# A gated MLP's down-projection by seven block products instead of eight

## The chip, the cores and the metric

The kernel runs on one core of a Trainium2 chip. The core has five engines with an instruction queue each: TensorE (PE in the profile; PEld is its loading of the stationary operand), VectorE (DVE), ScalarE (ACT), GpSimd (POOL) and SyncE (SP), which here only issues DMA transfers. The metric is the device time of one execution in microseconds, the median of several runs.

## The reference

One layer of an encoder: 512 tokens, 1024 channels, float32. A mixer with two branches fills the first two thirds of the kernel; the change is behind it, in the channel sublayer and the two layer norms around it:

```python
x = layer_norm(ALPHA * x + merged @ w_out[l], ln1_g[l], ln1_b[l])
u = causal_dwconv(x @ w_up[l], f_conv_w[l], f_conv_b[l])      # width 3, x is 512 x 1024, w_up 1024 x 5504
u_gate, u_val = jnp.split(u, 2, -1)                            # 512 x 2752 each
x = layer_norm(ALPHA * x + (jax.nn.silu(u_gate) * u_val) @ w_down[l], ln2_g[l], ln2_b[l])   # w_down 2752 x 1024
```

## The kernel before

**Precision.** A float32 matrix product is made of three products of a narrower float type, `fp32r`. Each operand X is split into a high part (`H`, ScalarE's cast) and a low part (`L` = X - H, a subtraction by VectorE), and TensorE adds H·H, L·H and H·L up in PSUM.

**Weights.** All weights lie in DRAM as units of 128x1024 (512 KB), in the order in which they are used. `advance(n)` keeps the stream ahead: SyncE loads `raw` up to four units ahead (`RAW_AHEAD`), and ScalarE and VectorE split units into `wH` and `wL` up to two ahead (`HL_AHEAD`); `raw`, `wH` and `wL` have rings of a few buffers. So each split waits for TensorE's last use of the buffer that it writes into.

**Up-projection.** For each of 21 blocks j of 128 channels, two units (gate and value) are multiplied into a PSUM bank each (`feature_major`, 24 matmuls of 128x512). `conv_taps` reads a bank three times (ScalarE, then two passes of VectorE), ScalarE applies silu, VectorE multiplies gate and value, and the result, channels x tokens, is split into `fH[j]` and `fL[j]`, which stay in SBUF. The last 64 channels of gate and value share one unit and one bank, `um`, and are read by the taps `cgm`.

**Down-projection.** `wide_product` holds 4 row blocks c of 128 tokens times 2 column halves hf, that is all 8 PSUM banks, `wd00` to `wd31`. For each block of 128 channels it does 24 matmuls with `fH`/`fL` as stationary operand and the split weights as moving one (`step`). The 16 first units run one after the other over all banks; the last five and the stacked 64 rows are done bank by bank, so that the row blocks end one after the other. PSUM banks come from two rings, `mm_bank` (to which `um` also belongs) and `sm_bank`.

**Around it.** After the first layer norm the normalised rows go to DRAM (`x1d`). For the residual, eight tiles `x1r[c][hf]` of 128x512 are read back ahead of the down-projection, and VectorE applies the first norm's scale `gt1[0]` and shift `gt1[1]`. When a bank is done, VectorE adds ALPHA times `x1r` (L1090) and takes statistics (L1091). `ln_finish` and `shift` make mean and deviation (GpSimd's power, L232, then `nb`, L1100), ScalarE normalises, VectorE multiplies with `gt2[0]`, GpSimd adds `gt2[1]`, SyncE stores. For the last row block, VectorE itself does most of this (L1122, L1124).

**Order.** A scheduler places the instructions on their engines; inside `in_order(*CORE)` they stand as written.

## Time and profile before

| | |
|---|---|
| median of 3 runs | 942.83 us (942.66 to 943.1) |
| profiled execution | 942.7 us, its span 941.0 us |
| granted TensorE clock | 0.994 of full speed, mean over the span |
| TensorE busy | 924.0 us of the span, 4565 matmuls |
| VectorE busy | 555.0 us, 916 instructions |
| ScalarE busy | 382.3 us |
| GpSimd busy | 66.0 us, 81 instructions |
| DMA | 105.13 MB, mean 112 GB/s |
| down-projection, first to last matmul's start | 812.69 to 931.42 us |

The busy time of an engine counts its running instructions alone. Matmuls overlap: each is shown with some 390 ns, but the next one starts earlier, so TensorE's time is best read from the distance of their starts. Rows name the engine, the line, and the tiles written and read. In this text, L numbers of the kernel before are those of its listing above; the changed kernel has its own.

### The profile page before, as it was taken

To read this page: it belongs to the slowest core of one execution; us is meant where nothing else is said; L and a number is where in the kernel's file an instruction comes from. 1 tells how busy PE (TensorE), PEld (TensorE's weight loads), DVE (VectorE), ACT (ScalarE), POOL (GpSimd) and SP (SyncE) were. 2 spreads that over 40 slices of the span, in tenths; PEclk is the share of its full clock that TensorE was granted. 3 is DMA by queue.
4 is the path that set the end of the run, shared out by engine and by line. 5 is a ranking of instruction groups with operands and counts; after the bars stand their busy time and mean duration, and the time that the engine had idled before them with its cause. 6 is when DMAs were issued, how large, how long until landed. Compare 5 with 4: busy or idle time off the path is not lost.

```text
span 941.0 us, 11703 instructions
## 1 busy us (share of the span) xinstructions
PE 924.0 (98%) x4565; PEld 762.3 (81%) x4565; DVE 555.0 (59%) x916; ACT 382.3 (41%) x572; POOL 66.0 (7%) x81
## 2 busy tenths in 40 slices
...
GB/s 186 105 101 138 109 88 142 123 147 118 90 111 70 139 109 77 102 90 96 106 112 157 112 178 91 90 90 92 109 90 93 110 90 91 251 128 90 95 62 90
DMA packets 46311, 105.13 MB, mean 112 GB/s; under 512 B 4064, under 2 KB 21144, under 8 KB 46256
## 3 DMA queue, kind: packets, MB, share of 16 engines
...
q0 software_dynamic: 512, 1.07, 0.4%
...
q14 instruction: 19, 0.16, 0.1%
...
HBM read 100.08 MB, written 4.30 MB: 111 GB/s over the span
## 4 chain that ended last, share of the span: by engine, by line
PE 94%; DVE 2%; DMA 1%; issue 1%; POOL 0%; ACT 0%; DVEq 0%; ACTq 0%; POOLq 0%
PE u L185 23%; PE wd L944 10%; PE g L185 9%; PE z L185 5%; PE o L185 5%; PE v L575 5%; PE xs L185 5%; PE pb L185 5%; PE pa L185 5%; PE wo L944 4%; PE bc L185 4%; PE q L185 2%; PE k L185 2%; PE bc L335 1%; PE up L185 1%
## 5 line engine op out<-in xcount | busy, mean ns | idle before, releaser
L165 DVE TENSOR_TENSOR wL<-raw,wH 128x1024 fp32r<-128x1024 f32 x151 | 186.4, 1238 | 231.3 <-ACT wH L159 229.2
L159 ACT CAST wH<-raw 128x1024 fp32r<-128x1024 f32 x152 | 159.1, 1051 | 285.5 <-PE g L185 62.8
L185 PE MATMUL u<-x1H,wL 128*128 128x512 f32 x312 | 121.4, 389 | 0.0
L185 PE MATMUL u<-x1L,wH 128*128 128x512 f32 x312 | 121.4, 389 | 0.0
L185 PE MATMUL u<-x1H,wH 128*128 128x512 f32 x312 | 121.4, 389 | 0.0
L185 PEld LDWEIGHTS u<-x1H,wH 128*128 128x128 f32 x312 | 58.6, 188 | 12.1
L185 PEld LDWEIGHTS u<-x1H,wL 128*128 128x128 f32 x312 | 58.6, 188 | 12.0
L185 PEld LDWEIGHTS u<-x1L,wH 128*128 128x128 f32 x312 | 58.6, 188 | 11.8
L944 PE MATMUL wd<-wH,fH 128*128 128x512 f32 x168 | 65.5, 390 | 0.8 <-ACT wH L159 0.8
L944 PE MATMUL wd<-wH,fL 128*128 128x512 f32 x168 | 65.4, 389 | 0.0
L944 PE MATMUL wd<-wL,fH 128*128 128x512 f32 x168 | 63.9, 389 | 0.0
L185 PE MATMUL g<-xnH,wH 128*128 128x512 f32 x128 | 50.1, 392 | 0.0
L185 PE MATMUL g<-xnH,wL 128*128 128x512 f32 x128 | 49.8, 389 | 0.0
L185 PE MATMUL g<-xnL,wH 128*128 128x512 f32 x128 | 49.8, 389 | 0.0
L232 POOL TENSOR_TENSOR rs<-ve,mhalf 128x1 f32<-128x1 f32 x12 | 7.6, 629 | 555.8 <-DVE ve L256 555.5
L944 PEld LDWEIGHTS wd<-wH,fH 128*128 128x128 f32 x168 | 31.5, 188 | 7.7 <-ACT wH L159 1.2
L944 PEld LDWEIGHTS wd<-wH,fL 128*128 128x128 f32 x168 | 31.5, 188 | 6.6
L944 PEld LDWEIGHTS wd<-wL,fH 128*128 128x128 f32 x168 | 31.5, 188 | 6.5
L1053 ACT CAST fH<-cg 128x512 fp32r<-128x512 f32 x21 | 13.0, 620 | 53.0 <-DVE cg L1051 53.0
L507 DVE SCALAR_TENSOR_TENSOR cv<-u,par,cv 128x511 f32<-128x511 f32 (+1 forms) x40 | 29.8, 746 | 0.7
L1050 ACT ACTIVATE cg<-cg 128x512 f32<-128x512 f32 x21 | 13.3, 632 | 40.8 <-DVE cg L507 40.8
L507 DVE SCALAR_TENSOR_TENSOR cg<-u,par,cg 128x511 f32<-128x511 f32 (+1 forms) x38 | 28.4, 746 | 0.6
...
## 6 DMA issues: line engine op xcount, KB each, us to landing
raw<-in_wts_dram SPq DMA_DIRECT2D x154, 512.0 KB, 3.3
csb<-scr SPq DMA_DIRECT2D x8, 512.0 KB, 7.3
gt<-in_prow_dram SPq DMA_DIRECT2D x12, 256.0 KB, 4.7
xt<-in_x_dram SPq DMA_DIRECT2D x4, 512.0 KB, 6.5
rb<-scr SPq DMA_DIRECT2D x4, 512.0 KB, 5.5
res<-in_x_dram SPq DMA_DIRECT2D x4, 512.0 KB, 5.3
x1d<-res SPq DMA_DIRECT2D x4, 512.0 KB, 2.6
x1r<-x1d SPq DMA_DIRECT2D x8, 256.0 KB, 5.7
```

The costliest lines, as they stand in the source:

```text
L159: nc.scalar.copy(H, raw)
L165: eng.tensor_tensor(L, raw, H.bitcast(F32), ALU.subtract)
L185: nc.tensor.matmul(ps[:, t0:t1], w_[:, k, :], a_[k][:, t0:t1], start=i == 0, stop=i == 3 * KD - 1)
L232: nc.gpsimd.tensor_tensor(dst, var, epsl[:, :n], ALU.pow)
L335: nc.tensor.matmul(fb[u][:, t], w_[:, k, :], a_[k][:, t], start=n == 1, stop=n == 3 * KD)
L507: nc.vector.scalar_tensor_tensor(dst[:, d:], ps[:, 0:T - d], prm(ws[n - 1 - d], j)[rows], dst[:, d:], ALU.mult, ALU.add)
L575: nc.tensor.matmul(banks[c], a_[k][:, cs_], w_[:, kk, :], start=first and s == 0, stop=last and s == 2)
L944: nc.tensor.matmul(banks[c, hf], a_[:, cs_], w_, start=k == 0 and s == 0, stop=k == n - 1 and s == len(prs) - 1)
L1050: nc.scalar.activation(tg, tg, AF.Silu)
L1053: nc.scalar.copy(H, tg)
```

## The change

The down-projection's 20 full blocks of 128 channels are cut in two halves of ten (K), the tokens in two halves of 256 (two row blocks each) and the output columns in two halves of 512. With A the activations and B the weights, eight block products A·B of these halves would be needed; the new code makes seven (Winograd's form of Strassen's method), from sums of blocks. A product p is 5 steps (p,i), each of 256 channels: 12 matmuls for two banks. Steps ("r",0) and ("r",1) are the remaining 128 and 64 channels, done plainly with 24 and 16 matmuls.

| p | activations | weights | banks | used for |
|---|---|---|---|---|
| 2 | A12 (`a2`) | B21 | `wdy` | rows 0-1, columns 0 |
| 1 | A11 (`a11`) | B11 | `wdx` | rows 0-1, columns 0 |
| 5 | s1 = A21 - A22 | B11 + B12 | `wdz` | rows 2-3, columns 1 |
| 6 | s2 = s1 - A11 | B11 + B12 + B22 | `wdx`, on top of 1 | rows 0-1, columns 1 |
| 3 | s4 = A12 + s2 | B22 | `wdz`, on top of 5 | rows 0-1, columns 1 |
| 7 | s3 = A11 - A21 | B12 + B22 | `wdx`, on top of 1 and 6 | rows 2-3, both halves |
| 4 | A22 (`a2`) | all four added | `wdw` | rows 2-3, columns 0 |

- *Sums of activations.* `UP_ORDER` makes the up-projection do blocks j and j + 10 in turn, so that GpSimd can form s1, s2 and s3 in float32 there (`sums`). A21 is kept no longer; A11, A12 and A22 are split at once. s4 is added up during product 5, first part by GpSimd, second part by VectorE, over s1. s1 to s4 are split right before use into `sr`, two pairs of tiles (`sr0`/`sr1`, `sr2`/`sr3`).
- *Sums of weights.* For product 1 ten tiles `tt` of 128x512 (256 KB) are loaded. As soon as a tile is split, GpSimd's queue issues a transfer that adds the next block from DRAM onto it: `tt` serves products 1, 5, 6 and 4 in turn, three additions for each. Product 7's tiles `dn7i` (512 KB) are loaded with B22, and B12 is added onto them.
- *Residual.* The first norm's scale and shift are applied on the way in four iterations of the up-projection (`residual`, two passes of 1024 columns per row block), through DRAM (`x1e`).
- *Order.* Within `in_order(ET.PE)` only TensorE's order is fixed as written; `ahead(n)` loads weights three steps ahead, splits them two ahead, splits sums one ahead. The banks are added onto `x1r` in pieces when a product is done (`scaled` for the first piece, `plus` for later ones). Row blocks 0 and 1 are finished during product 7; the last two steps of product 4 are done for row block 2, then for row block 3, in written order.

The diff's core:

```diff
+UP_ORDER = [j for i in range(10) for j in (i, i + 10)] + [20]
...
+    def residual(c):
+        t = ff.tile([P, 1024], F32, tag="raw", name=f"x1a{c}", bufs=1)
+        nc.sync.dma_start(t, x1d[:, c, :])
+        nc.vector.tensor_tensor(t, t, g1, ALU.mult)
+        nc.vector.tensor_tensor(t, t, b1, ALU.add)
+        nc.sync.dma_start(x1e[:, c, :], t)
+
+    for i, j in enumerate(UP_ORDER):
+        tg = gated(i, j)
+        if i in (3, 5, 7, 9):
+            residual((i - 3) // 2)
+        if j < 10:
+            low = tg
+            split(a11[j // 2][0][:, j % 2, :], a11[j // 2][1][:, j % 2, :], tg[:, 0:TH])
+        elif j < 20:
...
+            nc.gpsimd.tensor_tensor(s1, low[:, TH:], tg[:, TH:], ALU.subtract)
+            nc.gpsimd.tensor_tensor(s2, s1, low[:, 0:TH], ALU.subtract)
+            nc.gpsimd.tensor_tensor(s3, low[:, 0:TH], low[:, TH:], ALU.subtract)
...
-    wd_tail = wide_product(UX["DN"], fH, fL, 5, "wd", last_stack=True)
+    bX, bY = ([mm_bank(f"wd{n}{i}") for i in range(2)] for n in "xy")
+    bZ, bW = ([sm_bank(f"wd{n}{i}") for i in range(2)] for n in "zw")
+    sr = [rp.tile([P, 2, TH], F32R, tag="r", name=f"sr{i}") for i in range(4)]
...
+    BANK = {1: bX, 2: bY, 3: bZ, 4: bW, 5: bZ, 6: bX, 7: bX}
+    SUM = {5: 0, 6: 1, 7: 2, 3: 0}
+    steps = ([(2, 0), (2, 1), (2, 2), ("r", 0), ("r", 1), (2, 3), (2, 4)] + [(1, i) for i in range(5)]
+             + [(5, i) for i in range(5)]
+             + [(6, 0), (6, 1), (3, 0), (6, 2), (3, 1), (6, 3), (3, 2), (6, 4), (3, 3), (3, 4)]
+             + [(7, i) for i in range(5)] + [(4, i) for i in range(5)])
...
+        if p == 7:
+            nc.gpsimd.dma_start(raw, block(0, 1, i), accum_op=ALU.add)
...
+            nxt = {1: (0, 512), 5: (10, 512), 6: (10, 0)}.get(p)
+            for q in range(2):
+                t = tt[2 * i + q]
+                split(H[:, q, :], L[:, q, :], t)
+                if nxt:
+                    k0, o = nxt
+                    nc.gpsimd.dma_start(t, wts[DN[k0 + 2 * i + q]][:, o:o + 512], accum_op=ALU.add)
+
+    def sum_step(p, i):
+        if p in (5, 6, 7, 3):
+            n = at_["srn"]
+            at_["srn"] += 1
+            H, L = sr[2 * (n % 2)], sr[2 * (n % 2) + 1]
+            split(H, L, sums[i][:, SUM[p], :, :])
+            shl[p, i] = H, L
+        if p == 5:
+            s4, a12 = sums[i][:, 0, :, :], [t[:, :, 0:TH].bitcast(F32) for t in a2[i]]
+            nc.gpsimd.tensor_tensor(s4, a12[0], sums[i][:, 1, :, :], ALU.add)
+            nc.vector.tensor_tensor(s4, s4, a12[1], ALU.add)
+
+    def ahead(n):
+        for what, f, m in (("load", load_step, n + 3), ("hl", split_step, n + 2), ("s", sum_step, n + 1)):
+            while at_[what] <= min(m, len(steps) - 1):
+                f(*steps[at_[what]])
+                at_[what] += 1
...
+    with in_order(ET.PE):
+        for n, (p, i) in enumerate(steps[:-2]):
+            ahead(n)
+            product(p, i)
+            if (p, i) == ("r", 1):
+                scaled(bX, 0, 1)
+                scaled(bZ, 2, 1)
+            elif (p, i) == (2, 4):
+                scaled(bY, 0, 0)
+            elif (p, i) == (1, 4):
+                plus(bX, 0, 0)
+                for c in range(2):
+                    stats2(c, 0)
+            elif (p, i) == (5, 4):
+                plus(bZ, 2, 1)
+            elif (p, i) == (6, 4):
+                plus(bX, 0, 1, op=ALU.subtract)
+            elif (p, i) == (3, 4):
+                plus(bZ, 0, 1)
+                for c in range(2):
+                    stats2(c, 1)
+            elif p == 7 and i < 2:
+                apply2(i)
+            elif (p, i) == (7, 4):
+                plus(bX, 2, 1, op=ALU.subtract)
+                scaled(bX, 2, 0)
...
+    with in_order(*CORE):
+        for c in (2, 3):
+            for p, i in steps[-2:]:
+                product(p, i, (c - 2,))
+            plus(bW, 2, 0, (c - 2,))
+            nc.vector.bn_stats(bn2[c][:, 0, :], x1r[c][0])
+            ln_finish(bn2[c], mv2[:, c, :], rs2[:, c:c + 1], f"2_{c}")
+            if c == 2:
+                apply2(c)
```

The order shows where this puts the instructions. First TensorE where the down-projection begins. Before, within the first unit's pass over the banks (tile names carry their kernel's numbers):

```order
L944 MATMUL wd21_6588<-wH132_6449,fH0_5004 128x512
L944 MATMUL wd21_6588<-wH132_6449,fL0_5005 128x512
L944 MATMUL wd21_6588<-wL132_6450,fH0_5004 128x512
L944 MATMUL wd31_6590<-wH132_6449,fH0_5004 128x512
L944 MATMUL wd31_6590<-wH132_6449,fL0_5005 128x512
L944 MATMUL wd31_6590<-wL132_6450,fH0_5004 128x512
L944 MATMUL wd00_6583<-wH133_6494,fH1_5043 128x512
L944 MATMUL wd00_6583<-wH133_6494,fL1_5044 128x512
L944 MATMUL wd00_6583<-wL133_6495,fH1_5043 128x512
```

After `wd21` comes `wd31`: the matmuls of `wd30`, whose buffer is that of `um`, stand further back, within the third unit. After the change, from the last matmul of `um`:

```order
L178 MATMUL um_6522<-x1H7_4412,wL131_6458 128x512
L1215 MATMUL wdy0_6589<-dnH20_6617,a2H0_5064 128x512
L1215 MATMUL wdy0_6589<-dnH20_6617,a2L0_5065 128x512
L1215 MATMUL wdy0_6589<-dnL20_6618,a2H0_5064 128x512
L1215 MATMUL wdy1_6590<-dnH20_6617,a2H0_5064 128x512
L1215 MATMUL wdy1_6590<-dnH20_6617,a2L0_5065 128x512
L1215 MATMUL wdy1_6590<-dnL20_6618,a2H0_5064 128x512
L1215 MATMUL wdy0_6589<-dnH20_6617,a2H0_5064 128x512
L1215 MATMUL wdy0_6589<-dnH20_6617,a2L0_5065 128x512
```

The fourth matmul of the new step (2,0) goes to `wdy1`, which has the buffer of `um`; the step's matmuls stand directly behind those of `um`, in written order.

Second, VectorE at the same place. Before, around the two taps that read `um`:

```order
L507 SCALAR_TENSOR_TENSOR cgm_6522<-um_6491,par_76,cgm_6522 128x511
L1078 TENSOR_TENSOR x1r01_6545<-x1r01_6545,gt111_6539 128x512
L1077 TENSOR_TENSOR x1r11_6553<-x1r11_6553,gt101_6535 128x512
L1077 TENSOR_TENSOR x1r20_6557<-x1r20_6557,gt100_6533 128x512
L1077 TENSOR_TENSOR x1r21_6561<-x1r21_6561,gt101_6535 128x512
L1078 TENSOR_TENSOR x1r10_6549<-x1r10_6549,gt110_6537 128x512
L1077 TENSOR_TENSOR x1r30_6565<-x1r30_6565,gt100_6533 128x512
L507 SCALAR_TENSOR_TENSOR cgm_6522<-um_6491,par_76,cgm_6522 128x510
L1077 TENSOR_TENSOR x1r31_6569<-x1r31_6569,gt101_6535 128x512
```

After:

```order
L1054 TENSOR_TENSOR dnL22_6626<-dn22_6613,dnH22_6625 128x1024
L500 SCALAR_TENSOR_TENSOR cgm_6547<-um_6522,par_76,cgm_6547 128x511
L1054 TENSOR_TENSOR sr1_6596<-sum0_5004,sr0_6595 128x512
L1054 TENSOR_TENSOR sr3_6598<-sum1_5005,sr2_6597 128x512
L500 SCALAR_TENSOR_TENSOR cgm_6547<-um_6522,par_76,cgm_6547 128x510
L1054 TENSOR_TENSOR dnLr0_6644<-dnr0_6615,dnHr0_6643 128x1024
```

The residual's passes are gone from between the taps; a split of 1024 weight columns now stands ahead of the first tap, and two splits of activation sums between the taps.

Third, VectorE at product 7's second step and at the kernel's end. At step (7,1), after the change:

```order
L1054 TENSOR_TENSOR dnL71_7208<-dn71_7183,dnH71_7207 128x1024
L1054 TENSOR_TENSOR sr3_6598<-sum0_5004,sr2_6597 128x512
L1227 TENSOR_TENSOR x1r01_6559<-x1r01_6559,wdz0_6591 128x512
L1227 TENSOR_TENSOR x1r11_6563<-x1r11_6563,wdz1_6592 128x512
L1230 BN_STATS bn2_0_6583<-x1r01_6559 128x6
L1054 TENSOR_TENSOR dnL72_7241<-dn72_7204,dnH72_7240 128x1024
L1230 BN_STATS bn2_1_6584<-x1r11_6563 128x6
L1054 TENSOR_TENSOR sr1_6596<-sum1_5005,sr0_6595 128x512
```

Two evacuations of `wdz` and a statistic stand between the split for (7,1) and the one for (7,2); before, no such work stood between two splits of weights. At the end, before:

```order
L1100 SCALAR_TENSOR_TENSOR nb2_2_7252<-mv2_6581,rs2_6582 128x1
L1090 SCALAR_TENSOR_TENSOR x1r30_6565<-x1r30_6565,wd30_6589 128x512
L1091 BN_STATS bn2_3_7123<-x1r30_6565 128x6
L1108 TENSOR_TENSOR x1r20_6557<-x1r20_6557,gt200_6573 128x512
L1108 TENSOR_TENSOR x1r21_6561<-x1r21_6561,gt201_6575 128x512
L1090 SCALAR_TENSOR_TENSOR x1r31_6569<-x1r31_6569,wd31_6590 128x512
L1091 BN_STATS bn2_3_7123<-x1r31_6569 128x6
L254 BN_AGGR mv2_6581<-bn2_3_7123 128x2
L256 TENSOR_SCALAR ve2_3_7295<-mv2_6581 128x1
L1100 SCALAR_TENSOR_TENSOR nb2_3_7298<-mv2_6581,rs2_6582 128x1
```

And after:

```order
L1227 TENSOR_TENSOR x1r20_6565<-x1r20_6565,wdw0_6593 128x512
L1285 BN_STATS bn2_2_6585<-x1r20_6565 128x6
L247 BN_AGGR mv2_6581<-bn2_2_6585 128x2
L249 TENSOR_SCALAR ve2_2_7430<-mv2_6581 128x1
L1239 SCALAR_TENSOR_TENSOR nb2_2_7433<-mv2_6581,rs2_6582 128x1
L1247 TENSOR_TENSOR x1r20_6565<-x1r20_6565,gt200_6573 128x512
L1247 TENSOR_TENSOR x1r21_6567<-x1r21_6567,gt201_6575 128x512
L1227 TENSOR_TENSOR x1r30_6569<-x1r30_6569,wdw1_6594 128x512
L1285 BN_STATS bn2_3_6586<-x1r30_6569 128x6
L247 BN_AGGR mv2_6581<-bn2_3_6586 128x2
L249 TENSOR_SCALAR ve2_3_7458<-mv2_6581 128x1
L1239 SCALAR_TENSOR_TENSOR nb2_3_7461<-mv2_6581,rs2_6582 128x1
```

Before, `nb` of row block 2 stood ahead of both additions of block 3, with block 2's two multiplications between them; now its statistics, power, `nb` and its two multiplications stand between the two blocks' last additions.

More of the change, by code (lines that the diff above doesn't have):

```diff
@@ L72, in unit_list @@
         add("WO", "rows", "w_out", 128 * k)
-    for j in range(21):
+    for j in UP_ORDER:
         add("UG", "cols", "w_up", 128 * j)
@@ L76, in unit_list @@
     add("UM", "mixed")
-    for k in range(21):
+    add("DR", "rows", "w_down", 128 * 20)
+    add("DR", "last")
+    for k in range(20):
         add("DN", "rows", "w_down", 128 * k)
-    add("DN", "last")
     return u, ix
@@ L129, in trunk @@
     EXTRA[UX["UG"][1]] = ("at", "bc", "bc", 3)
-    EXTRA.update({u: ("ff", "xw", "xw", 4) for u in UX["DN"][-2:]})
+    STREAM_END = UX["UM"][0]
     def advance(n, hl=HL_AHEAD):
-        while st["raw"] <= min(n + RAW_AHEAD, len(UNITS) - 1):
+        while st["raw"] <= min(n + RAW_AHEAD, STREAM_END):
             u = st["raw"]
@@ L138, in advance @@
             st["raw"] += 1
[L139 removed]
+        while st["hl"] <= min(n + hl, STREAM_END):
             u = st["hl"]
```

159 lines of the change are left out of this document (109 added, 50 removed).

## The prediction

> **What bounds the kernel now.** I read the engine totals and the chain first, then the stages by windows, then single rows.
>
> ```profile
> PE 924.0 (98%) x4565; PEld 762.3 (81%) x4565; DVE 555.0 (59%) x916; ACT 382.3 (41%) x572; POOL 66.0 (7%) x81
> PE 94%; DVE 2%; DMA 1%; issue 1%; POOL 0%; ACT 0%; DVEq 0%; ACTq 0%; POOLq 0%
> ```
>
> TensorE holds 94% of the chain that ends last. The windows are the up-projection, the down-projection and the tail; the columns are the engines' busy time (with instruction counts), granted clock, DMA share and GB/s.
>
> ```profile
> core 0: us, PE busy (x) PEld busy (x) DVE busy (x) ACT busy (x) POOL busy (x), PEclk, DMA share, GB/s
> 600.00:812.00 212.00, 212.00 (x936) 175.55 (x935) 132.94 (x162) 93.18 (x120) 0.95 (x1) 1.00 0.29 97
> 812.70:931.60 118.90, 118.12 (x521) 97.33 (x519) 51.90 (x71) 27.83 (x31) 8.13 (x8) 1.00 0.34 118
> 931.60:941.00 9.40, 0.20 (x1) 0.00 (x0) 4.96 (x9) 0.60 (x1) 4.57 (x5) 0.75 0.30 112
> ```
>
> The down-projection is 118.9 us of dense matmuls, with VectorE busy for 51.9 of them. A matmul's 389 ns overlap with the next one's, so the price is the distance of starts:
>
> ```profile
> 812.69 0.39 PE L944 MATMUL wd<-wH,fH 128*128 128x512 f32 x1
> 838.26 0.39 PE L944 MATMUL wd<-wH,fH 128*128 128x512 f32 x1
> ...
> 840.52 0.39 PE L944 MATMUL wd<-wH,fL 128*128 128x512 f32 x1
> 840.75 0.39 PE L944 MATMUL wd<-wL,fH 128*128 128x512 f32 x1
> 840.95 1.05 ACT L159 CAST wH<-raw 128x1024 fp32r<-128x1024 f32 x1 [4.21 <-PE wd L944]
> 840.98 0.39 PE L944 MATMUL wd<-wH,fH 128*128 128x512 f32 x1
> 842.04 1.22 DVE L165 TENSOR_TENSOR wL<-raw,wH 128x1024 fp32r<-128x1024 f32 x1 [4.04 <-ACT wH L159]
> 931.42 0.39 PE L944 MATMUL wd<-wL,fHm 128*128 128x512 f32 x1
> ```
>
> Twelve matmuls run from 838.26 to 840.98: 2.72 us, 0.227 each. The 520 of the stage need 519 x 0.227 = 117.7 us from first start to last; it took 118.7, so 1.0 us is waiting. The rows also give the handover that the rest is built on: ScalarE's cast starts 0.03 us before the next step's first matmul (its buffer is last read one matmul earlier), takes 1.05, and VectorE follows 0.04 later. For VectorE and its neighbours back to back:
>
> ```profile
> 824.61 3.10 DVE L1078 TENSOR_TENSOR x1r<-x1r,gt 128x512 f32<-128x512 f32 x5
> 829.93 3.50 DVE L165 TENSOR_TENSOR wL<-raw,wH 128x1024 fp32r<-128x1024 f32 x3 [0.26 <-ACT wH L159]
> L149 ACT CAST wH<-raw 128x512 fp32r<-128x512 f32 x2 | 1.2, 617 | 4.6 <-DMA raw<-in_wts_dram 4.6
> L1090 DVE SCALAR_TENSOR_TENSOR x1r<-x1r,wd 128x512 f32<-128x512 f32 x8 | 5.5, 688 | 8.3 <-PE wd L944 8.3
> 928.20 1.53 ACT L1115 ACTIVATE x1r<-x1r,nb,rs 128x512 f32<-128x512 f32 x2 [4.83 <-DVE nb L1100]
> ```
>
> Five operations of 512 columns last 3.10, so each further one costs 0.60 and the last ends after 0.69; of 1024 columns, 1.14 and 1.22.
>
> **The change, part by part.** *Matmuls removed.* Eight block products of 60 become seven: 35 steps of 12, and 40 for the last 192 rows: 460 instead of 520. 60 x 0.227 = **-13.6 us**; the wait of 1.0 goes with the old order: **-1.0**.
>
> *Start of the down-projection.* Now step (2,0) uses both `wdy` banks within four matmuls, and `wdy1` is the buffer of `um`, the last up-projection bank. Before, the scheduler put the product that needs it behind the first two units.
>
> ```profile
> L505 ACT ACTIVATE cgm<-um,par x1: 767/767/767, 813.6 to 813.6; 128x512 f32<-128x512 f32 x1
> L507 DVE SCALAR_TENSOR_TENSOR cgm<-um,par,cgm x2: 743/744/744, 819.1 to 823.4; 128x511 f32<-128x511 f32 x1, 128x510 f32<-128x510 f32 x1
> ```
>
> `um` was read until 824.1 and nobody waited. In the new order, from the end of `um`: ScalarE casts until 1.02 us, VectorE's split of 1024 columns goes from 1.06 to 2.20, the first tap to 2.86, two splits of `sum` to 4.06, the second tap ends at 4.80. The fourth matmul could start at 0.68, and starts at 4.87: **+4.2 us**. TensorE idles from 0.84 on, for 4.0 us. What that does to its clock:
>
> ```profile
> 1.51 6.33 PE L211 MATMUL warm<-wz 128*128 128x512 bf16 x22 [1.51 <-DVE wz L206]
> 11.00:12.00 1.00, 0.40 (x1) 0.18 (x1) 0.56 (x2) 0.00 (x0) 0.96 (x1) 0.62 1.02 418
> 13.50:17.00 3.50, 3.50 (x16) 3.32 (x17) 2.52 (x7) 2.29 (x6) 1.11 (x2) 0.50 0.15 60
> 17.00:18.00 1.00, 1.00 (x3) 0.29 (x2) 0.63 (x3) 1.00 (x4) 0.90 (x1) 0.50 0.00 0
> 18.00:19.00 1.00, 1.00 (x7) 0.72 (x6) 1.00 (x2) 1.00 (x5) 1.00 (x1) 0.97 0.00 0
> 936.00:937.00 1.00, 0.00 (x0) 0.00 (x0) 1.00 (x2) 0.00 (x0) 0.92 (x2) 0.62 0.00 0
> ```
>
> After the warm-up matmuls end at 7.84, the mean clock of 0.62 between 11 and 12 puts the fall to 0.5 at 11.24, 3.4 us later; after the last matmul (end 931.81) it falls at 936.24, 4.4 us later. From 13.5 it takes 4.5 us of work to come back, which costs 2.2. An idle of 4.0 lies between 3.4 and 4.4: bounds 0 and 2.2, taken near the half, **+1.0**. The Trainium skill (TensorE: Matmul & The Clock Gate, on what is actually happening) says that the clock falls after one idle window of some 3.4 us that runs freely. By it an idle of 4.0 us holds a whole window in about one case of six, an estimate that would make the term 0.4 and the sum 941.4.
>
> *Steps of 2.72 us instead of units of 5.44.* Every step splits 1024 weight columns, and from (5,0) to (7,4) also 512 of `sum` into `sr`, whose two pairs come free only when the step two earlier has ended; the low part is wanted at the step's start. Each line below counts VectorE's queue from the end of that earlier step, where 2.72 is due:
> - (5,2): counted from the end of (1,4), with 5.44 due: 0.21 + 2 adds, 2 statistics, 4 half splits (8 x 0.60) + 0.69 + 0.05 = 5.75, late 0.3.
> - (6,0): 0.63 (a half cast) + two halves and an addition for s4 (1.80) + 0.69 + 0.05 = 3.17, late 0.45.
> - (6,1): from 0.31, 2 adds 1.20, split 1.14, s4 0.60, 0.69, 0.05 = 3.99, against 3.17: 0.8.
> - (6,2), (6,3), (6,4) and (7,3): -0.03 + 1.05 + 0.04 + 1.14 + 0.69 + 0.05 = 2.94, late 0.22 each: 0.9. A late step gives the next one room, so only every second one counts.
> - (3,4): 0.21 + two subtractions 1.20 + 1.14 + 0.69 + 0.05 = 3.29: 0.6.
> - (7,1): the same with two adds and two statistics, 4.49: 1.8.
> - (7,4): four activations of 0.765 stand before its cast; worked through both queues: 1.5.
>
> Sum **+6.3 us**. As a floor, VectorE's work in steps (5,0) to (5,4) and (7,0) to (7,4), at 0.69 an operation 15.2 and 15.8 us for 13.6 each, makes 3.8.
>
> *Tail.* Row block 2 now ends one step before block 3, and its normalisation stands ahead of block 3's on every queue.
>
> ```profile
> 930.82 2.82 POOL L1109 TENSOR_TENSOR x1r<-x1r,gt 128x512 f32<-128x512 f32 x2 [2.85 <-DVE x1r L1108]
> 931.84 0.69 DVE L1090 SCALAR_TENSOR_TENSOR x1r<-x1r,wd 128x512 f32<-128x512 f32 x1 [0.56 <-PE wd L944]
> 933.77 0.55 POOL L232 TENSOR_TENSOR rs<-ve,mhalf 128x1 f32<-128x1 f32 x1
> 934.35 0.16 DVE L1100 SCALAR_TENSOR_TENSOR nb<-mv,rs 128x1 f32<-128x1 f32 x1 [0.66 <-POOL rs L232]
> ```
>
> From these rows, `nb` follows the add by 2.51. Block 2's add starts at -2.51 (0 is the last step's end), `nb` ends at 0.16, two activations end at 1.73, the second multiplication runs until 2.45, and block 3's add starts at 2.37 instead of 0.21. GpSimd's two additions (2.82) then hold the power until 4.57, 0.27 past its time. **+2.4 us**.
>
> *Transfers.* 30 accumulating ones of 256 KB and five of 512 KB are new, on GpSimd's queue; no row shows an accumulating one.
>
> ```profile
> raw<-in_wts_dram SPq DMA_DIRECT2D x154, 512.0 KB, 3.3
> csb<-scr SPq DMA_DIRECT2D x8, 512.0 KB, 7.3
> rsb<-rsd POOLq DMA_DIRECT2D x4, 256.0 KB, 4.2
> L862 POOL DMA_DIRECT2D rsb<-rsd x4 | 3.0, 765 | 2.3 <-DMA rsd<-rs_y 2.3
> ```
>
> Issue is 0.77; landing is bounded by 3.3 and 7.3. I take some 5 (4.2 for half the bytes, issued from the same queue). The tightest of the first set is issued 14.6 us before (5,0)'s turn less 5.5: 9.1 us. For (7,2) to (7,4) the buffer, a load of 3.3, the issue and the accumulation follow each other, and 6.2 us are left for the last. So **0**, up to 1.1 with 7.3; below nothing is excluded, as no transfer was removed from the path.
>
> *Up-projection.* GpSimd's 30 sums (0.95 us busy in 212 before), VectorE's eight passes of 1.22 for the residual (132.94 of 212) and SP's two loads of 512 KB plus four each way for it (DMA share 0.29) have room; weights are split a unit and a half ahead, so a late weight load behind them has 5 us to spare. 0. The 16 multiplications and additions they replace, and four loads, lay beside matmuls.
>
> Sum: 942.7 (the profiled execution: span 941.0 and 1.7 around it; the median is 0.1 more) - 13.6 - 1.0 + 4.2 + 1.0 + 6.3 + 2.4 = **942.0 us**.
>
> **Rivals.** *Only VectorE's total counts*: the single waits melt into each other, 3.8 for 6.3, and the clock holds: 938.5, and 936 if the start also costs less. For it: VectorE rests for 4.2 us of a unit today. Against: queues are in order, and its new order is fixed.
>
> *Accumulating transfers are late* (the other side): it decides at 6.2 us for 512 KB, at (7,2). If an addition doubles some 5 to 10, (7,2) waits 4 and (5,0) one: 947; at 3 times, 955. For it: weights are now fetched twice, 21 MB in 104 us instead of 11; against: four transfers from GpSimd flew together. The Trainium skill (Collectives: The Full Stack, on the bandwidth ceiling) has adding at about half the copy rate, since it reads two sources. No run here shows it.
>
> *VectorE and GpSimd block each other* while s4 is added (GpSimd, three times beside VectorE):
>
> ```profile
> L677 POOL TENSOR_TENSOR y<-y,yo 128x512 f32<-128x512 f32 x6 | 11.6, 1927 | 67.0 <-DVE yo L676 67.0
> L289 DVE TENSOR_TENSOR xnL<-xnf,xnH 128x256 fp32r<-128x256 f32 x16 | 7.3, 506 | 0.0
> L289 DVE TENSOR_TENSOR x1L<-x1f,x1H 128x256 fp32r<-128x256 f32 x16 | 6.7, 420 | 1.1
> ```
>
> Blocking for three whole additions of 1.44 (L1109's pair above) is 4.3 us: 946.3. GpSimd's went up to 1.93 beside VectorE and one split from 420 to 506 ns, so rather 1 us. The Trainium skill (SBUF — State Buffer, on who interferes with whom) says the second to issue fully blocks; the trace agrees only in part.
>
> **How the numbers follow.** A run tells 0.2%, 1.9 us, from no change. The forecast (940.9 to 944.7) has 0.35, VectorE's total 0.32, late transfers 0.25, blocking 0.08. Low terms 942.7 - 14.6 + 3.5 + 3.8 + 1.9 = 937.3; high 942.7 - 14.6 + 6.4 + 9.3 + 2.6 = 946.4. From 936 to 951 leaves out the larger transfer delays and a gain near the full 14.6: 0.2. The forecast's own range is 939 to 945.
>
> **What would show it.** Right: 460 `wd` matmuls; a gap of about 4 us after `um` with the last release by `cgm`; waits of TensorE for `sr` at (6,1), (7,1), (7,4); block 3's `nb` 5 us after the last matmul. Wrong: waits for accumulating transfers, or a down-projection under 110 us from first start to last.

## The result and the profile after

| | before | after |
|---|---|---|
| median | 942.75 us (942.29 to 943.1, 4 runs) | 951.99 us (950.45 to 952.61, 4 runs) |
| profiled execution | 942.7 us | 952.06 us, its span 950.3 |
| down-projection, first to last matmul's start | 812.69 to 931.42 us | 812.72 to 937.31 us |

The ratio of the times is 1.0096, with a 95% interval from 1.0078 to 1.0113: slower by 1%, where 942.0 and no change were forecast. It is 7 us above the forecast's own range of 939 to 945, and 1 us above the wide one of 936 to 951.

The page's totals and its chain, after:

```profile
PE 917.9 (97%) x4505; PEld 753.5 (79%) x4505; DVE 602.2 (63%) x979; ACT 407.0 (43%) x626; POOL 134.8 (14%) x151
PE 91%; DVE 3%; DMA 3%; issue 2%; ACT 1%; POOL 1%; DVEq 0%; ACTq 0%; POOLq 0%
```

The 60 matmuls are gone (4565 to 4505), but TensorE's share of the chain fell from 94 to 91%, and DMA has 3% of it. What TensorE waited for from 800 us on, in the view of waits (engine, tile written, releaser, then total us, times, longest):

```profile
PE wdx L1215 <- DVE sr L1054: 7.2, 4, 5.0
PE wdx L1215 <- ACT sr L1053: 4.4, 2, 4.2
PE wdz L1215 <- DVE sr L1054: 1.2, 2, 0.6
```

Of these 12.8 us, 9.2 are two waits, of 4.2 and 5.0 us, both for `sr`. The windows show where; their columns are the engines' busy time, granted clock, DMA share and GB/s:

```profile
812.60:835.30 22.70, 22.70 (x102) 18.81 (x101) 18.38 (x23) 11.10 (x15) 7.73 (x7) 1.00 1.00 338
835.30:849.00 13.70, 13.70 (x63) 11.33 (x62) 7.86 (x13) 5.75 (x11) 8.87 (x11) 1.00 1.08 183
849.00:863.00 14.00, 12.82 (x55) 9.97 (x54) 13.10 (x18) 7.75 (x14) 10.97 (x12) 1.00 1.05 177
863.00:892.00 29.00, 27.58 (x118) 21.31 (x117) 22.02 (x29) 14.41 (x21) 10.30 (x11) 1.00 0.95 196
892.00:922.00 30.00, 19.74 (x66) 14.63 (x65) 19.97 (x27) 11.69 (x17) 11.39 (x9) 0.79 0.54 127
```

Products 2 and 1 run without a gap. From 849 us (product 5) TensorE has small gaps, and in product 7 (892 to 922) it is busy for 19.74 of 30 us at a mean clock of 0.79. Next to the clock stands the DMA share, the time of all packets added up, as a share of 16 engines' time (so it can pass 1). It is 0.95 to 1.08 from 812 to 892 us, which is called full here, though from 835 on the DMA engines move only 177 to 196 GB/s, where plain loads at 812 to 835 had moved 338.

From the starts of all 460 matmuls in the trace I took for each step what it lasted beyond 0.2265 us a matmul; a wait ahead of a step is booked to the step before it. These excesses are used below for every run:

| steps | excess, us |
|---|---|
| (5,3), (5,4), (6,0), (6,1) | 0.90, 0.94, 1.21, 0.82 |
| (3,4), (7,0), (7,1) | 4.55, 3.48, 0.66 |
| (7,4) | 7.05 |
| all others together | 1.0 |

The sum of 20.6 holds 12.8 of waits (the three rows above); of the other 7.8 some 4.4 are the lower clock behind the two long waits, where the starts are some 0.42 apart instead of 0.2265, and the rest are small gaps. It adds up: 942.7 - 13.6 - 1.0 + 20.6 + 3.4 (tail) = 952.1.

**The wait ahead of (7,0).** Rows of SyncE, GpSimd, ScalarE, VectorE and TensorE; the brackets give the idle time before and its releaser:

```profile
879.74 0.37 SPq L1148 DMA_DIRECT2D dn<-in_wts_dram  x1
889.22 1.20 POOL L1150 DMA_DIRECT2D dn<-in_wts_dram  x1 [5.67 <-DMA dn<-in_wts_dram]
896.97 1.04 ACT L1053 CAST dnH<-dn 128x1024 fp32r<-128x1024 f32 x1 [6.86 <-DMA dn<-in_wts_dram]
897.92 0.61 ACT L1053 CAST sr<-sum 128x512 fp32r<-128x512 f32 x1
898.04 1.23 DVE L1054 TENSOR_TENSOR dnL<-dn,dnH 128x1024 fp32r<-128x1024 f32 x1 [6.50 <-ACT dnH L1053]
898.59 0.49 PE L1215 MATMUL wdx<-dnH,sr 128*128 128x512 f32 x1 [4.19 <-ACT sr L1053]
```

This is the tile of step (7,1), `dn71`. Its load is issued at 879.74, when its buffer comes free; GpSimd waits for the load and issues the addition at 889.22. ScalarE's cast of `dn71` waits for the addition and starts at 896.97, 17.2 us after the first issue. Behind that cast in ScalarE's queue stands the cast of (7,0)'s `sr`. So TensorE waits at (7,0) for the weights of (7,1), though (7,0)'s own are there: the row names `sr`, but the late one is a transfer.

**The wait in (7,4).**

```profile
910.96 4.68 DVE L1247 TENSOR_TENSOR x1r<-x1r,gt 128x512 f32<-128x512 f32 x4
911.72 6.70 POOL L1248 TENSOR_TENSOR x1r<-x1r,gt 128x512 f32<-128x512 f32 x4 [2.99 <-DVE x1r L1247]
915.56 3.41 DVE L1054 TENSOR_TENSOR dnL<-tt,dnH 128x512 fp32r<-128x512 f32 x2
919.63 0.80 PE L1215 MATMUL wdx<-dnH,sr 128*128 128x512 f32 x1 [4.98 <-DVE sr L1054]
```

While GpSimd adds `gt2[1]` for row blocks 0 and 1, VectorE's four multiplications take 4.68 us and the next two splits 3.41. Before, such operations were 0.6 apart (2.5 and 1.3). Two of VectorE's and two of GpSimd's, one by one:

```profile
911.72 1.68 POOL L1248 TENSOR_TENSOR x1r<-x1r,gt 128x512 f32<-128x512 f32 x1 [2.99 <-DVE x1r L1247]
912.17 1.79 DVE L1247 TENSOR_TENSOR x1r<-x1r,gt 128x512 f32<-128x512 f32 x1
913.37 1.72 POOL L1248 TENSOR_TENSOR x1r<-x1r,gt 128x512 f32<-128x512 f32 x1
913.88 1.75 DVE L1247 TENSOR_TENSOR x1r<-x1r,gt 128x512 f32<-128x512 f32 x1
```

The first two multiplications, started ahead of GpSimd, last 0.68 and 0.69. The third starts while GpSimd's first addition runs and ends at 913.96, 0.55 behind that addition's end; the fourth ends 0.55 behind the second addition, and the two splits 0.55 behind the other two. So each of them is held until GpSimd's addition is done, and loses 1.1 us. VectorE's split of `sr` for (7,4) stands behind them.

**The tail.**

```profile
939.34 2.97 POOL L1248 TENSOR_TENSOR x1r<-x1r,gt 128x512 f32<-128x512 f32 x2 [1.84 <-DVE x1r L1247]
939.88 0.68 DVE L1227 TENSOR_TENSOR x1r<-x1r,wdw 128x512 f32<-128x512 f32 x1
942.84 0.16 DVE L1239 SCALAR_TENSOR_TENSOR nb<-mv,rs 128x1 f32<-128x1 f32 x1 [1.12 <-POOL rs L225]
```

Block 3's last addition starts 2.57 us behind the last matmul's start (0.42 before) and `nb` 5.53 behind it (2.93 before). From that start to the span's end it is 13.0 us, against 9.6 before: 3.4 more.

### The profile page after: what moved, and what is told of

Same layout as the page of the kernel before. It is cut to its first block, busy times and chain, and to the rows that moved or that the text cites. A ratio compares the mean times of both kernels' runs of the same rounds, so it can differ in the third digit from the quotient of the medians.

```text
span 950.3 us, 11910 instructions
## 1 busy us (share of the span) xinstructions
PE 917.9 (97%) x4505; PEld 753.5 (79%) x4505; DVE 602.2 (63%) x979; ACT 407.0 (43%) x626; POOL 134.8 (14%) x151
## 4 chain that ended last, share of the span: by engine, by line
PE 91%; DVE 3%; DMA 3%; issue 2%; ACT 1%; POOL 1%; DVEq 0%; ACTq 0%; POOLq 0%
PE u L178 22%; PE g L178 9%; PE z L178 5%; PE o L178 5%; PE v L568 5%; PE xs L178 5%; PE pa L178 5%; PE pb L178 5%; PE wo L937 4%; PE bc L178 3%; PE wdx L1215 3%; PE q L178 2%; PE k L178 2%; DMA dn<-in_wts_dram 2%; PE wdy L1215 1%
## 5 line engine op out<-in xcount | busy, mean ns | idle before, releaser
L158 DVE TENSOR_TENSOR wL<-raw,wH 128x1024 fp32r<-128x1024 f32 x131 | 162.2, 1241 | 168.9 <-ACT wH L156 166.9
L156 ACT CAST wH<-raw 128x1024 fp32r<-128x1024 f32 x131 | 137.1, 1049 | 229.3 <-PE g L178 62.8
L1215 PE MATMUL wdx<-dnH,sr 128*128 128x512 f32 x80 | 29.8, 448 | 11.7 <-DVE sr L1054 7.2
L1053 ACT CAST dnH<-tt 128x512 fp32r<-128x512 f32 x40 | 22.8, 618 | 35.8 <-PE wdx L1215 19.0
L1054 DVE TENSOR_TENSOR dnL<-tt,dnH 128x512 fp32r<-128x512 f32 x40 | 30.4, 796 | 9.3 <-ACT dnH L1053 9.2
L1215 PEld LDWEIGHTS wdx<-dnH,sr 128*128 128x128 f32 x80 | 17.2, 215 | 18.8 <-DVE sr L1054 9.8
L1171 POOL DMA_DIRECT2D tt<-in_wts_dram x30 | 26.9, 1004 | 29.5 <-DVE dnL L1054 18.3
L1054 DVE TENSOR_TENSOR dnL<-dn,dnH 128x1024 fp32r<-128x1024 f32 x15 | 18.3, 1222 | 18.0 <-ACT dnH L1053 18.0
L178 PEld LDWEIGHTS g<-xnH,wL 128*128 128x128 f32 x128 | 24.0, 188 | 5.0
```

The costliest lines, as they stand in the source:

```text
L156: nc.scalar.copy(H, raw)
L158: eng.tensor_tensor(L, raw, H.bitcast(F32), ALU.subtract)
L178: nc.tensor.matmul(ps[:, t0:t1], w_[:, k, :], a_[k][:, t0:t1], start=i == 0, stop=i == 3 * KD - 1)
L1053: nc.scalar.copy(H, t)
L1054: nc.vector.tensor_tensor(L, t, H.bitcast(F32), ALU.subtract)
L1171: nc.gpsimd.dma_start(t, wts[DN[k0 + 2 * i + q]][:, o:o + 512], accum_op=ALU.add)
```

## The experiments

**Each suspect by itself.** Four edits of the changed kernel take one suspect away each. In e1 the 30 transfers that add onto `tt` become plain ones of the same size, issued at the same places; in e6 the five for product 7:

```diff
-                    nc.gpsimd.dma_start(t, wts[DN[k0 + 2 * i + q]][:, o:o + 512], accum_op=ALU.add)
+                    nc.gpsimd.dma_start(t, wts[DN[k0 + 2 * i + q]][:, o:o + 512])
```

> The 30 transfers onto the tt tiles overwrite instead of adding (so products 5, 6 and 4 use single blocks of weights); bytes, queue, order and waits are those of the changed kernel. Theory A (an adding packet of 2 KB takes 178 ns of a DMA engine where a plain one takes 84, the DMA engines are full from 822 to 880 us, and the load of product 7's second tile, 9.2 us, is late for that): with plain ones the wait of 4.4 us ahead of step (7,0), the 1.1 behind it and the 3.0 us that the halved clock cost there go: 943.5 us (942 to 945). Theory B (product 7's own chain, buffer free, load, issue, addition, is too long whatever else is on the DMA engines): nothing changes, 952.

Measured: 948.83 us, ratio 1.0065 [1.0048, 1.0082], 3.2 less than after the change. That is between the two. The excess of (3,4), the wait ahead of (7,0), went from 4.55 to 0.39, but (7,1) now has 3.32; of 8.7 in (3,4), (7,0) and (7,1), 5.6 stayed. The windows of product 5, and of 6 and 3:

```profile
849.00:863.00 14.00, 13.41 (x58) 10.46 (x57) 13.10 (x18) 7.80 (x14) 8.81 (x13) 1.00 0.54 185
863.00:892.00 29.00, 28.04 (x120) 21.69 (x119) 21.00 (x29) 14.69 (x22) 7.88 (x11) 1.00 0.71 198
```

The same bytes (185 GB/s against 177) take the DMA engines half the time: a share of 0.54 instead of 1.05. So adding cost twice as much DMA time as copying here. The Trainium skill (Collectives: The Full Stack, on the bandwidth ceiling) has that ratio for additions between cores, and these two rows agree with it for an addition from DRAM onto a tile.

> The five transfers onto product 7's tiles overwrite instead of adding (product 7 uses B12 alone); all else is as in the changed kernel. Theory A: the load of the second tile is still late, only its second transfer gets shorter, from 7.7 us to about 5: the wait ahead of (7,0) falls from 4.4 to some 1.6, and the clock perhaps keeps: 945.5 to 949 us. Theory B: the same link of the chain is halved: also 946 to 949, so it is the tt run that tells A from B, and this one prices the link.

Measured: 947.99 us, ratio 1.0055 [1.004, 1.007], as expected. (3,4), (7,0) and (7,1) have 1.77, 1.26 and 1.44, so 4.5 of 8.7 stayed here too. With either set of additions plain, more than half of the waits stays.

e4 leaves out GpSimd's additions of `gt2[1]` for row blocks 0 and 1:

```diff
-            nc.gpsimd.tensor_tensor(x1r[c][hf], x1r[c][hf], gt2[1][hf], ALU.add)
+            if c == 2:
+                nc.gpsimd.tensor_tensor(x1r[c][hf], x1r[c][hf], gt2[1][hf], ALU.add)
```

> GpSimd's four additions of gt2[1] for row blocks 0 and 1 are left out (their rows lack the second norm's shift); all else stands as in the changed kernel. Theory C (VectorE's multiplications and splits beside them take twice as long, 4.68 us for four and 3.41 for two, and that makes most of the wait of 5.3 us in step (7,4)): the four take 2.5, the two 1.3, the wait falls to about 1 us and the halved clock behind it (1.8) goes: 945.5 us (944.5 to 947). Theory D (the place in the queues alone, four activations and four multiplications ahead of the split): 950 to 952, a wait of 3 us or more stays.

Measured: 945.34 us, ratio 1.0029 [1.0019, 1.0039], 6.65 less, as expected. VectorE's rows at the same place:

```profile
910.57 2.49 DVE L1247 TENSOR_TENSOR x1r<-x1r,gt 128x512 f32<-128x512 f32 x4
912.98 1.29 DVE L1054 TENSOR_TENSOR dnL<-tt,dnH 128x512 fp32r<-128x512 f32 x2
```

The same instructions take 2.49 and 1.29 us instead of 4.68 and 3.41, and (7,4)'s excess falls from 7.05 to 1.52, which is the 1.5 that the prediction had for it.

h1 does the same to the additions for s4 during product 5, cut to 32 of 256 columns (`s4[:, :, 0:32]`):

> GpSimd's additions for s4 are cut to 32 of 256 columns (product 3 uses partly wrong sums); the rest is the changed kernel, but that in two steps VectorE's half of s4 stands one place earlier. Theory C for product 5 (the 3.9 us of waits from (5,3) to (6,1) are partly VectorE's operations running slower beside these 1.6 us additions): the waits fall to the 1.5 us that the prediction's working gave without that, 949.5 to 950.5 us. If the queue's length alone makes them: 951.5 to 952.5.

Measured: 949.18 us, ratio 1.0075 [1.006, 1.009], 2.8 less and just below the 949.5 to 950.5 of theory C. The interval overlaps that of the changed kernel (1.0078 to 1.0113), so the steps have to show it: (5,3) to (6,1) go from 0.90, 0.94, 1.21, 0.82 to 0.50, 0.19, 0.23, 0.25. The operations that this frees are these three in the trace after the change, held by additions of GpSimd that end at 856.90, 859.92 and 863.88, each 0.55 or 0.56 before VectorE's:

```profile
855.66 1.79 DVE L1054 TENSOR_TENSOR dnL<-tt,dnH 128x512 fp32r<-128x512 f32 x1
858.58 1.91 DVE L1054 TENSOR_TENSOR dnL<-tt,dnH 128x512 fp32r<-128x512 f32 x1
862.21 2.23 DVE L1183 TENSOR_TENSOR sum<-sum,a2L 128x512 f32<-128x512 f32 x1
```

Against the usual 0.69, VectorE loses 3.9 us in them.

**The start's wait, made on purpose.** After the change TensorE does not wait for the taps that read `um`, which the prediction had priced at 5.2 us with the clock. Its rows, and the last tap's, after the change:

```profile
813.40 0.39 PE L1215 MATMUL wdy<-dnH,a2H 128*128 128x512 f32 x1
816.78 0.74 DVE L500 SCALAR_TENSOR_TENSOR cgm<-um,par,cgm 128x510 f32<-128x510 f32 x1
```

The first is the fourth matmul of (2,0), the one into `wdy1`; it starts 3.4 us before the last read of `um` and waits for nothing. `wdy1` does not have the buffer of `um`, as the text ahead of the prediction says: in the program as built that buffer went to `wdx1`, which is first written at 821 us. (No trace names buffers; that the row above waits for nothing agrees with it.) e5 gives it to `wdy1`:

```diff
-    bX, bY = ([mm_bank(f"wd{n}{i}") for i in range(2)] for n in "xy")
+    bX, bY = [mm_bank(f"wdx{i}") for i in range(2)], [mm_bank("wdy0"), pg]
```

> The second bank of product 2 is made the very tile um, so that its first matmul must wait for the second tap that reads um (one other bank stays unused). The prediction had this by assumption. Its working (first possible start 0.68 us behind um, second tap ends 4.80 us behind it) gives a gap of 4.2 us and 0 to 2.2 for the clock: 956 to 958.5 us. The other way: the wait gives VectorE and the DMA engines time that they lack later, and the later waits shrink by as much: 952 to 954.

Measured: 958.28 us, ratio 1.0164 [1.0149, 1.018], 6.3 more, within the expected range.

```profile
817.79 0.56 PE L1215 MATMUL um<-dnH,a2H 128*128 128x512 f32 x1 [4.11 <-DVE cgm L500]
```

And its window behind that wait:

```profile
818.00:820.00 2.00, 2.00 (x6) 1.52 (x6) 1.85 (x2) 0.99 (x2) 1.35 (x2) 0.51 1.00 382
```

The wait is 4.1 us (4.0 was worked out), and the clock is 0.51 behind it, to 821.4 us: (2,0) has 5.95 more, 4.3 of it between the two starts (4.2 was worked out) and 1.7 by the clock (1.0 was taken, from bounds of 0 and 2.2). The arithmetic was right; the clash was not there.

**Is it the order?** Four kernels write out the order on all engines, with the normalisation of row blocks 0 and 1 moved behind (4,0) and (4,1). f0 keeps the change's order of a step (split of the next weights, split of the sums, then the banks' additions). f5 puts the sums and the banks ahead of the weights. f6 issues product 4's 10 additions onto `tt` later, behind product 7's. f1 does both.

```diff
-            ahead('hl', n + 2)
             ahead('s', n + 1)
             evac(*steps[n - 1]) if n else None
+            ahead('hl', n + 2)
...
-            nxt = {1: (0, 512), 5: (10, 512), 6: (10, 0)}.get(p)
+            nxt = {1: (0, 512), 5: (10, 512)}.get(p)
...
+        if p == 4:
+            for q in range(2):
+                nc.gpsimd.dma_start(tt[2 * i + q], wts[DN[10 + 2 * i + q]][:, 0:512], accum_op=ALU.add)
```

> All engines but SP take the down-projection's instructions in written order: per step the split of weights two ahead, the split of a sum one ahead, then the additions of the bank last ended; row blocks 0 and 1 are normalised behind steps (4,0) and (4,1) instead of in product 7; VectorE's half of s4 follows one step later; product 7's loads may start four steps ahead. This is the base for the next three. Both theories: the wait in (7,4) with its slow clock goes (7.4 us), that ahead of (7,0) stays (8 to 9 us with the clock): 944 to 947 us.

> As the written order, but each step's sum is split ahead of the weights of the step after it. Theory E (ScalarE's queue: the sum for (7,0) stands behind the cast of (7,1)'s tile, which waits for its addition; the late tile alone would have a step to spare): the wait ahead of (7,0) goes and only 1 to 2 us each are left at (7,1) and (7,2): 4 to 6 us less than the written order. Theory A (DMA engines full, the tiles late by more than a step): the wait moves to (7,1) nearly whole, 0 to 2 us less.

> As the written order, but the ten last additions onto tt (for product 4) are issued behind those onto product 7's tiles. Theory A: product 7's loads and additions then have the DMA engines for themselves, its tiles land 4 us or more earlier, and 4 to 7 us are saved against the written order. Theory B (its own chain of load, issue and addition, some 12 us from the release of a buffer, is too long): no more than 2 us are saved.

> Both edits of the two runs before. If A and E each have a part, nearly all of the 8 to 9 us in product 7 goes: 935 to 938 us, faster than before the change. If B holds, 940 or more.

Measured: f0 966.05 (1.025 [1.0235, 1.0265]), f5 955.03 (1.0132 [1.0115, 1.0149]), f6 961.12 (1.0201 [1.0185, 1.0216]), f1 951.78 (1.0097 [1.0081, 1.0112]). f0 missed by far, and f1 came out in the range given for theory B: writing out the order brought waits of its own. In f0 this one makes 9.8 us in (7,1):

```profile
910.44 0.56 POOL L225 TENSOR_TENSOR rs<-ve,mhalf 128x1 f32<-128x1 f32 x1 [9.85 <-DVE ve L249]
911.46 0.56 POOL L225 TENSOR_TENSOR rs<-ve,mhalf 128x1 f32<-128x1 f32 x1 [0.46 <-DVE ve L249]
912.02 2.45 POOL L1186 DMA_DIRECT2D dn<-in_wts_dram  x2
```

GpSimd's queue waited 9.85 us for the statistics of a row block, with product 7's additions behind. Against f0, the order of the splits gives 11.0 us (4 to 6 were expected), the later additions 4.9 (4 to 7), both 14.3. In f1 the waits at (3,4), (7,0) and (7,1) are gone (0, 0 and 0.30 left); others came in their place ((5,4) 2.89, (7,2) 5.83, (7,3) 2.85, the last two steps of product 4 for row block 2 6.93). The longest of them is again for a late tile of product 7, whose addition GpSimd issues at 901.33, behind its power for two row blocks:

```profile
907.03 1.04 ACT L1053 CAST dnH<-dn 128x1024 fp32r<-128x1024 f32 x1 [6.98 <-DMA dn<-in_wts_dram]
```

So f1 moves the wait and doesn't tell what forces it; the order matters, but these four don't separate it from the transfers.

**All suspects at once, and what was left.** h2 (`h2_three` in the expectations) joins the edits of e1, e6, e4 and h1.

> All three edits that leave work out at once, in the changed kernel: plain transfers for all 35 accumulating ones, GpSimd's additions for row blocks 0 and 1 left out, those for s4 cut. If DMA additions, and GpSimd beside VectorE, are the whole of the loss against the matmuls' saving, then 952 less 8.7 at (7,0) and (7,1), 7.4 at (7,4) and 2 in product 5: 933.5 to 935.5 us, and what is left above 928 is the tail and product 5's queue. If something else limits product 7: 938 or more.

Measured: 938.34 us, ratio 0.9948 [0.9932, 0.9965], 13.7 less, where the four edits by themselves sum to 16.6. It is not the 933.5 to 935.5 of an account that is complete, but the 938 or more of something else that limits product 7: (7,0) and (7,1) kept 1.54 and 3.22. Its rows:

```profile
887.99 0.73 POOL L1150 DMA_DIRECT2D dn<-in_wts_dram  x1 [6.07 <-DVE sr L1054]
893.21 1.05 ACT L1053 CAST dnH<-dn 128x1024 fp32r<-128x1024 f32 x1 [3.99 <-DMA dn<-in_wts_dram]
```

The load of `dn72` was issued at 881.66, when an earlier split released its buffer; the second transfer at 888; the cast could start at 893.21. That is 11.5 us from release to use, with plain transfers and a mean DMA share of 0.81 from 882 to 893. So the late buffer has a part of its own. i1 takes the after kernel and gives product 7's tiles, as halves, ten buffers that are free since product 1; i2 does so with h2:

```diff
+        if p == 7:
+            blk[p, i] = [ff.tile([P, 512], F32, tag="a11", name=f"dn7{i}{q}", bufs=10) for q in range(2)]
+            for q in range(2):
+                nc.sync.dma_start(blk[p, i][q], wts[DN[10 + 2 * i + q]][:, 512:1024])
+            for q in range(2):
+                nc.gpsimd.dma_start(blk[p, i][q], wts[DN[2 * i + q]][:, 512:1024], accum_op=ALU.add)
+            return
...
-        if p == 7:
-            nc.gpsimd.dma_start(raw, block(0, 1, i), accum_op=ALU.add)
```

> Only product 7's tiles move: each is two halves of 128x512 in ten buffers that nobody else uses any more (those of A11, last read by product 1), loaded and added in the same places of the written order as in the changed kernel. Theory B (the chain that starts with a buffer released late): loads no longer wait for a split two products back, both transfers land before they are wanted; the excess of (3,4), (7,0) and (7,1) goes from 8.7 to under 1 us: 943 to 944.5 us. Theory A (the adding transfers keep the DMA engines full, so that even early ones land late): a gain of at most 3 us, 949 to 952, and waits for dn<-in_wts_dram remain in ScalarE's rows. The 7.0 at (7,4) and product 5's 3.9 stay in both.

> The kernel h2_three (plain transfers for all 35, GpSimd's additions for row blocks 0 and 1 left out, s4's cut to 32 of 256 columns; not the reference's result), with the same free buffers for product 7. If the 4.9 us that were left at (3,4), (7,0) and (7,1) come from the late buffers (theory B): they fall under 0.5, 933 to 934.5 us. If they come from the queues of ScalarE and VectorE themselves: no change, 937.5 to 939.

Measured: i1 956.95 us, ratio 1.0157 [1.014, 1.0174], 5.0 **more** than after the change and above what either theory had; i2 936.0 us, ratio 0.9932 [0.9918, 0.9947], 2.3 less than h2 and between its two expectations. In i1 the waits ahead of and in (7,0) are gone: (3,4), (7,0) and (7,1) have 0.30, 0 and 1.24 instead of 4.55, 3.48 and 0.66. But (5,2) to (3,0) now have 14.7 together, where they had 3.9. ScalarE's longest wait in 849 to 884 us is for transfers onto `tt`:

```profile
ACT dnH L1053 <- DMA tt<-in_wts_dram: 10.6, 6, 4.2
```

i1's window of product 5, with the DMA share at 1.11 and 254 GB/s:

```profile
849.00:863.00 14.00, 10.72 (x45) 8.34 (x44) 7.15 (x12) 4.52 (x8) 9.25 (x11) 0.98 1.11 254
```

The page's row of the additions onto `tt`, with the median time from issue to landing last: after the change,

```profile
tt<-in_wts_dram POOLq DMA_DIRECT2D x30, 256.0 KB, 5.7
```

in i1,

```profile
tt<-in_wts_dram POOLq DMA_DIRECT2D x30, 256.0 KB, 10.4
```

and in i2, where they are plain:

```profile
tt<-in_wts_dram POOLq DMA_DIRECT2D x30, 256.0 KB, 4.7
```

With free buffers product 7's loads start at 838.07 us and its additions run from 845.7 to 872, between those for products 5 and 6 on GpSimd's queue and on full DMA engines, and those are late instead. In the change's order neither theory is enough alone: the late buffer puts the stall at (7,0), and with the buffer free the full DMA engines move it to product 5. With both away (i2) the down-projection has 4.9 us of excess left, 3.6 from (3,4) to (7,4); TensorE's waits there are for `sr`, and ScalarE has none for a transfer.

**A version without these waits.** g1 loads product 7's halves ten steps ahead into free buffers and adds six ahead; product 4's additions come five ahead, behind product 7's; s4 is formed early, by VectorE, into buffers of its own; row blocks 0 and 1 are normalised by two passes of VectorE, without GpSimd. All additions stay. g2 does the last three steps of product 4 row block by row block.

```diff
-                nc.gpsimd.tensor_tensor(s4, a12[0], sums[i][:, 1, :, :], ALU.add)
+        nc.vector.tensor_tensor(s4[i], aH, sums[i][:, 1, :, :], ALU.add)
...
-                apply2(APPLY[p, i])
+                direct2(APPLY[p, i])
...
+            nc.vector.scalar_tensor_tensor(t, t, mv2[:, c, 0:1], gt2[0][hf], ALU.subtract, ALU.mult)
+            nc.vector.scalar_tensor_tensor(t, t, rs2[:, c:c + 1], gt2[1][hf], ALU.mult, ALU.add)
```

> The same seven products in written order, with each cause taken away: product 7's tiles lie in buffers that product 1 leaves, so that their loads and additions start during product 6 and wait for no split; their additions stand ahead of product 4's on GpSimd's queue; a sum is split ahead of the next step's weights; s4 is added by VectorE alone, in the steps ('r',0) to (1,1), into buffers that product 2 leaves; row blocks 0, 1 and 2 are normalised by VectorE alone (two passes for each half) from (7,4) on, block 2 in the gaps of block 3's chain. If the causes are complete: 942.7 - 13.6 - 1.0 = 928 and up to 4 us for what is left in product 5 and the tail: 928 to 932 us. If the DMA engines are the bound whatever the order (some 95 us of transfers in 100): waits stay in products 7 or 4 and it takes 936 or more.

> As the run before, with the last three steps of product 4 (not two) done for row block 2 and then for block 3, so that block 2 ends 4.1 us ahead of block 3 instead of 2.7. If block 2's passes still delayed block 3: 0.5 to 1.5 us less; otherwise no difference, or a little more where the third step's weights must be ready earlier.

Measured: g1 932.72 us (932.65 to 932.8), ratio 0.9894 [0.9879, 0.9909]: 10.1 us faster than before the change, 19.3 faster than after it, and 0.7 above the 928 to 932 that were expected. g2 is at 934.81, 0.991 [0.9894, 0.9927], a miss: (6,0) to (3,0) have 1.2 of new waits, and product 4 has 5.0 of excess where g1 has 2.0. TensorE's only wait in g1 from 800 us on:

```profile
PE wdw L1246 <- DVE dnL L1054: 1.4, 2, 1.0
```

Its windows of product 5, and of 6 and 3:

```profile
849.00:863.00 14.00, 14.00 (x64) 11.58 (x63) 10.38 (x18) 8.03 (x15) 6.82 (x9) 1.00 1.11 251
863.00:892.00 29.00, 29.00 (x130) 24.01 (x129) 23.22 (x33) 17.72 (x28) 11.04 (x13) 1.00 1.05 208
```

The DMA engines are as full as after the change (1.11, 1.05), an addition onto `tt` takes almost as long to land as in i1 (9.7 against 10.4 us), and TensorE runs without a gap beside them:

```profile
tt<-in_wts_dram POOLq DMA_DIRECT2D x30, 256.0 KB, 9.7
```

Product 7's loads start at 838 here too, but its additions are issued at 861.5 to 875.3, behind those for products 5 and 6. So the full DMA engines cost nothing when each addition is issued early enough, in the order of use. (g1 takes away several causes at once; e4 and h1 price GpSimd's part by itself.) Of the 14.6 us that 60 matmuls and the old waits are worth, 2.0 stay in the steps of product 4, and 2.8 in the tail (12.4 us from the last start at 918.64 to the span's end, against 9.6).

## Why the prediction was wrong

- *Removed matmuls, -13.6, and the old order's wait, -1.0*: right. Where nothing waits (812.72 to 849), the steps start 2.72 us apart, and 460 matmuls are there.
- *Start, +4.2 and +1.0 for the clock*: failed in its premise. It took the banks of a ring to be given out in turn. The excess there is 0; e5 shows that with the clash the price would have been 5.95. This error hid part of the others, by luck: without it the sum was 936.8.
- *Transfers, 0*: one of the two large failed steps, 6.3 us (8.7 less the 0.6 and 1.8 that VectorE's queue was to cost at (3,4) and (7,1)). It took some 5 us for landing and a chain of load 3.3, issue, and 6.2 for the last. The load and the addition of `dn71` took 17.2 from issue to use, because additions keep the DMA engines twice as long, 35 of them fill the engines from 835 to 892 us, and the chain starts only when a buffer is released. It is the rival of late transfers, with (7,2) named as the place where it decides, and 947 to 955 us for it; the place was (7,1), whose cast holds up (7,0) in ScalarE's queue. The rule of the Trainium skill (Collectives: The Full Stack, on the bandwidth ceiling) that the prediction set beside this rival, about half the copy rate, was the better guide than the nearest rows, all of which were copies.
- *VectorE's queue, +6.3*: the other large failed step, 8.0 us ((7,4) 7.05 against 1.5, products 5, 6 and 3 4.3 against 2.2, (7,3) 0.55 against 0.2). The queue count was near and its durations were not. With GpSimd's tensor work and the late transfers away, i2 has 3.6 us from (3,4) to (7,4), where the prediction's terms are 0.6, 1.8, 0.2 and 1.5, and 1.3 in products 5, 6 and 3, where it had 2.2. What failed is the 0.60 us for an operation that starts beside one of GpSimd's: it lasts until 0.55 us behind the end of that one, 1.7 to 2.2 us. That turned the 1.5 at (7,4) into 7.05 (1.52 without it, in e4), and cost 2.7 from (5,3) to (6,1) (h1). The rival on VectorE and GpSimd had the mechanism, and its 4.3 us for three blocked operations is near the 3.9 that VectorE lost in product 5. The prediction looked at s4 alone, though by e4 and h1 the four additions in product 7 cost more than twice what s4's do. And it cut the 4.3 to 1 us by a mean: the 506 ns of its row are fifteen splits of 0.41 to 0.42 us and one that was held, in the trace before the change already:

```profile
17.10 2.37 POOL L165 TENSOR_TENSOR wL<-raw,wH 128x1024 fp32r<-128x1024 f32 x1 [2.13 <-ACT wH L157]
17.92 1.83 DVE L289 TENSOR_TENSOR xnL<-xnf,xnH 128x256 fp32r<-128x256 f32 x1
```

- *Tail, +2.4*: right in its mechanism, 3.4 measured. Block 3's addition came 2.15 later than before (2.16 were worked out), `nb` 2.96 behind it: GpSimd's power waits for its additions as worked out. The other 0.8 lies behind `nb`, where the prediction added nothing; the engines take the same 3.2 us from there to VectorE's last operation, so it lies in the last stores and the end of the program.
- *Up-projection, 0*: right. The first matmul of the down-projection starts at 812.72, before at 812.69.
- The account closes: -5.2 (start) + 6.3 (transfers) + 8.0 (VectorE beside GpSimd) + 1.0 (tail) = 10.1 us, from 942.0 to 952.1.
- Of what was to show it right, the waits for `sr` at (7,4) and `nb` 5 us behind the last matmul were there; the gap behind `um` was not. Waits for accumulating transfers, named as the sign that it is wrong, were there.

What stays open: how the 6.3 us at product 7's tiles divide between the late buffer, the additions' DMA time and GpSimd's queue, since the edits don't add up there, and whether the last 2.0 and the tail of g1 can be had.
